# An output projection by seven block products in place of eight, with differences of weight blocks made on GpSimd

## The chip, the cores and the metric

The kernel runs on one core of a Trainium2 chip. The metric is the device time of one execution in microseconds (us); less is better. The engines are named as in the profile: PE (TensorE, matmul; PEld are its weight loads), DVE (VectorE), ACT (ScalarE), POOL (GpSimd), SP (SyncE, which here issues all the DMAs, in program order).

## The reference, cut to what matters

One block of a decoder: x is 1024 tokens by 1024 channels, float32. Two branches, an mLSTM with 4 heads and an S5 state space, are merged by sigmoid gates and go through one output projection, a norm and a residual.

```
xn = rmsnorm(h, norm_pre_g[l])
proj = xn @ w_in[l]
...
y_a = mlstm_branch(...) @ w_a_out[l]
y_b = s5_branch(...) @ w_b_out[l]
g = jax.nn.sigmoid(g_pre.astype(jnp.float32)).astype(h.dtype)
merged = g[..., :D_MODEL] * y_a + g[..., D_MODEL:] * y_b
h = h + rmsnorm(merged @ w_o[l], norm_post_g[l])
```

The last line is what the change touches: merged and w_o are both 1024 by 1024.

## The kernel before, in words

**Products.** All large matmuls are made from float32 values that are split into a high and a low part in a reduced format (fp32r): `dot3` (L181 to L184) issues hi x hi, hi x lo and lo x hi for each 128-deep slice of the contraction. Splitting a value takes a copy on ScalarE (the high part) and a subtraction (the low part). Results gather in PSUM accumulators of 128 by 512: `bank()` hands out 3 of them (tag `pp`), `mbank()` 5 (tag `pm`).

**Weights.** `plan` lists the weight pieces in the order of use. `fetch` loads the next piece into raw tiles (`wr`), `pump` splits one piece into `wh` (ScalarE, L142) and `wl` (L144, on VectorE, or on GpSimd where asked), and `take` hands it over. There are two buffers each of `wr`, `wh` and `wl`.

**Order.** The order of the work is written out by hand. `run` plays one unit: it first issues the DMAs that wait in `pending` (`tick`; `store` puts one there), then the early loads of the next units in `fillers` (as many as `look` says), then the unit's body, and then what an earlier unit put off with `defer`, one unit late. `fill(n)` plays the next n units of `fillers`.

**The S5 output stage** (L780 to L860) has 8 gate units (`glu_unit`, L826: 12 matmuls, tanh on ScalarE, three steps on VectorE) and 16 output units (`yb_unit`, L837: 12 matmuls 128x512 into a `pm` accumulator, then one VectorE step, L844, with a 256 KB tile `aux`, and a store of the product to `gb_d` in DRAM). The tile `aux` is loaded three units ahead (L820) into one of six buffers; it is held until the store of its product has landed.

**The next projection** follows at once: `o_unit` (L895), whose first head makes 264 columns (24 matmuls per unit, `pp` accumulators). ScalarE takes 256 columns (`sow`, L902) and VectorE the other 8 (`gall`, L905), for which it needs two small bias loads (`bif`, L879, L880); these are issued on SyncE behind the last stores of the S5 output stage.

**The merge** (L1410 to L1510) finishes the mLSTM branch's projection and merges: four partial units of 18 matmuls (`ya_unit` with i = 3), sixteen merge units of 6 (`mg_unit`, L1425): one VectorE step on the accumulator (L1432), one that adds the other branch, a copy on ScalarE to `mh`, and one unit late a subtraction on GpSimd to `ml` (L1440). Merge units are named by row block of 128 channels and half of the tokens: (0,1) is block 0, second half.

**The output projection** (`wo_unit`, L1446) takes w_o in four pieces of 256 columns; each piece runs over 8 tiles of 128 tokens, 24 matmuls 128x256 in a unit, 768 in all. The units of the first piece are mixed with the last merge units. Behind each unit ScalarE squares the accumulator (L1460, for the norm), VectorE multiplies by the norm's weight, and in the last piece GpSimd makes the root (L1467, L1468) and VectorE scales and adds the residual (`finish`, L1474, two steps of 128x512), which is stored.

Of the kernel before, what the change touches and what calls it, by code (L numbers as in the profile page):

```python
# [36 lines left out]
def hybrid_block(ctx, tc, x, norm_pre_g, w_in, conv_w, conv_b, w_q, w_k, w_v, b_i, b_f, head_g,  # L37
# [780 lines left out]
    def load_aux(key, src):  # L818
        t = gq.tile([P, 512], F32, tag="aux", bufs=6, name="aux")
        SY.dma_start(t, src)  # L820
# [594 lines left out]
    mh, ml = {}, {}

    def mg_pre(ct, hf):
        rs = slice(ct * P, (ct + 1) * P)
# [4 lines left out]
        maux[ct, hf] = (t1, pr, None)

    def mg_unit(ct, hf):  # L1425
        if "ya3" not in cur:
# [5 lines left out]
        V.scalar_tensor_tensor(t1, t1, 1.0, o, op0=ALU.add, op1=ALU.mult)  # L1432
# [4 lines left out]
        mh[ct, hf] = fp.tile([P, 512], F32R, name=f"mh{ct}{hf}")  # L1437
        ml[ct, hf] = fp.tile([P, 512], F32R, name=f"ml{ct}{hf}")
        A.activation(mh[ct, hf], t1, AF.Copy)  # L1439
        defer(lambda: PL.tensor_tensor(ml[ct, hf], t1, mh[ct, hf].bitcast(F32), op=ALU.subtract))  # L1440

    ob, xres = {}, {}
    sso = fp.tile([P, NCH, 5], F32, name="sso")

    def wo_unit(i, t):
        if t == 0:  # L1446
            cur["wo", i] = take(("wo", i), i > 0)
        if i == 0:
            ob[t] = main.tile([P, D], F32, tag=f"xh{t}", name=f"ob{t}")
            xres[t] = main.tile([P, D], F32, tag=f"xl{t}", name=f"xr{t}")  # L1450
        if i == 1:
            SY.dma_start(xres[t], x[0, t * P:(t + 1) * P, :])
        hf = t // 4
        sl = slice((t % 4) * P, (t % 4 + 1) * P)
        o = bank()
        proj_tm(o[:, :256], lambda k: mh[k, hf][:, sl], lambda k: ml[k, hf][:, sl], cur["wo", i], 0, 256,
                KT)
        cs = slice(256 * i, 256 * (i + 1))
        jk = fp.tile([P, 256], F32, tag="fjk", bufs=1, name="fjk")
        A.activation(jk, o[:, :256], AF.Square, scale=1.0 / 32.0, accum_out=sso[:, t, i:i + 1])  # L1460
        mul(ob[t][:, cs], o[:, :256], gpo[:, cs])
        if i == 2:
            V.tensor_reduce(sso[:, t, 4:5], sso[:, t, 0:3], axis=mybir.AxisListType.X, op=ALU.add)
            V.tensor_scalar(sso[:, t, 4:5], sso[:, t, 4:5], 4.0 * EPS, None, op0=ALU.add)
        if i == 3:
            s = fp.tile([P, 1], F32, tag="fs", bufs=4, name="fs")
            PL.tensor_tensor(s, sso[:, t, 3:4], sso[:, t, 4:5], op=ALU.add)  # L1467
# [75 lines left out]
```

## Time and profile before

| what | us |
|---|---|
| runs | 989.50, 988.57, 987.05 |
| median | 988.57 |
| the profiled execution | 987.63 |
| its span, first to last instruction | 985.9 |

Rows of a timeline give start, duration, engine, line, operation, out<-in with shapes, and in brackets the idle time of the engine just ahead and what ended it. SPq rows are the queue of SyncE: the start is the issue of a DMA, not its landing. Rows of groups give the busy time, the mean of one in ns, and the idle time ahead of them with its releaser.

### The profile page before, as it was taken

The page shows a single profiled execution, that of the slowest core. Times are in us where ns is not written, and L with a number is a line of the kernel's source. Part 1 is how long each engine was busy: PE and PEld are TensorE (multiplying, and loading weights), DVE is VectorE, ACT ScalarE, POOL GpSimd, SP SyncE. Part 2 cuts the span into 40 slices and gives each one's busy share as a digit, 9 for nine tenths or more (in the row PEclk, how much of TensorE's full clock was granted, in tenths as well). Part 3 has the DMA queues.
Part 4 walks back from the last instruction along what each step waited for, and adds up shares of the span by engine and source line. Part 5 has one row for each costly group of instructions (what it writes and reads, how often), then busy time and mean ns, then how long its engine had stood idle before and what let it go on. Part 6 is the DMA issues. An engine that isn't in the chain of part 4 may idle for free.

```text
span 985.9 us, 15233 instructions
## 1 busy us (share of the span) xinstructions
PE 972.8 (99%) x5644; PEld 840.9 (85%) x5644; DVE 621.9 (63%) x1397; ACT 352.9 (36%) x697; POOL 207.1 (21%) x215
## 2 busy tenths in 40 slices
PE   9999999999999999999999999998999999999997
PEld 7888888888887889978998898888988888879997
DVE  5437968879644752444686677747775888664225
ACT  7413132231314421224544445434543452233211
POOL 3013122111112000013111321223222311462002
PEclk9999999999999999999999999999999999999999
DMA  7454323423434566115344254335437895772504
GB/s 257 109 159 150 96 89 99 111 57 110 110 97 166 186 216 229 59 68 148 97 134 152 82 178 124 134 97 177 133 117 226 281 302 191 243 249 90 193 1 172
DMA packets 113722, 145.17 MB, mean 147 GB/s; under 512 B 18888, under 2 KB 71280, under 8 KB 113648
## 3 DMA queue, kind: packets, MB, share of 16 engines
q1 hardware_dynamic: 113648, 144.21, 46.0%
q8 instruction: 44, 0.72, 0.3%
q14 instruction: 30, 0.25, 0.1%
HBM read 98.79 MB, written 45.38 MB: 146 GB/s over the span
## 4 chain that ended last, share of the span: by engine, by line
PE 88%; issue 3%; POOL 3%; DVE 2%; DMA 2%; ACT 1%; SPq 0%; DVEq 0%; POOLq 0%; ACTq 0%
PE pp L182 24%; PE pp L183 23%; PE pp L184 23%; PE pm L184 4%; PE pm L182 4%; PE pm L183 4%; PE pm L1151 1%; POOL wl L144 1%; PE pm L727 1%; PE pm L768 1%; PE pm L767 1%; PE pm L1074 1%; DMA so_d<-sow 1%; POOL ml L1440 1%; POOL t2k L1270 1%
## 5 line engine op out<-in xcount | busy, mean ns | idle before, releaser
L182 PE MATMUL pp<-xh,wh 128*128 128x512 f32 x768 | 306.9, 400 | 0.0
L183 PE MATMUL pp<-xl,wh 128*128 128x512 f32 x768 | 303.8, 396 | 0.0
L184 PE MATMUL pp<-xh,wl 128*128 128x512 f32 x768 | 303.8, 396 | 0.0
L182 PEld LDWEIGHTS pp<-xh,wh 128*128 128x128 f32 x768 | 144.4, 188 | 35.1 <-ACT wt L691 0.8
L184 PEld LDWEIGHTS pp<-xh,wl 128*128 128x128 f32 x768 | 144.4, 188 | 34.6
L183 PEld LDWEIGHTS pp<-xl,wh 128*128 128x128 f32 x768 | 144.5, 188 | 32.4 <-DVE xl L295 0.3
L144 POOL TENSOR_TENSOR wl<-wr,wh 128x1024 fp32r<-128x1024 f32 (+1 forms) x25 | 61.6, 2482 | 229.1 <-ACT wh L142 229.1
L142 ACT ACTIVATE wh<-wr 128x1024 fp32r<-128x1024 f32 (+2 forms) x74 | 71.0, 1006 | 46.5 <-PE pm L183 30.6
L184 PE MATMUL pp<-wh,ml 128*128 128x256 f32 x256 | 72.6, 284 | 1.3 <-POOL ml L1440 1.3
L144 DVE TENSOR_TENSOR wl<-wr,wh 128x1024 fp32r<-128x1024 f32 (+2 forms) x49 | 55.9, 1172 | 27.7 <-ACT wh L142 23.2
L182 PE MATMUL pp<-wh,xh 128*128 128x256 f32 (+1 forms) x256 | 72.3, 282 | 0.6 <-ACT sow L902 0.6
L183 PE MATMUL pp<-wl,mh 128*128 128x256 f32 x256 | 72.5, 283 | 0.0
L182 PE MATMUL pp<-wh,mh 128*128 128x256 f32 x256 | 71.9, 281 | 0.0
L184 PE MATMUL pp<-wh,xl 128*128 128x256 f32 (+1 forms) x256 | 71.8, 281 | 0.0
L183 PE MATMUL pp<-wl,xh 128*128 128x256 f32 (+1 forms) x256 | 71.8, 280 | 0.0
L308 ACT ACTIVATE tg<-pp 128x512 f32<-128x512 f32 x32 | 19.2, 598 | 127.4 <-PE pp L184 89.4
L1048 POOL TENSOR_TENSOR hll<-t2k,hlh 128x512 fp32r<-128x512 f32 x16 | 21.1, 1319 | 182.7 <-ACT hlh L1047 106.0
L184 PEld LDWEIGHTS pp<-wh,ml 128*128 128x128 f32 x256 | 48.1, 188 | 1.7 <-POOL ml L1440 1.7
L182 PEld LDWEIGHTS pp<-wh,mh 128*128 128x128 f32 x256 | 48.7, 190 | 0.5 <-ACT mh L1439 0.4
L182 PEld LDWEIGHTS pp<-wh,xh 128*128 128x128 f32 x256 | 48.1, 188 | 1.2 <-ACT sow L902 1.0
L183 PEld LDWEIGHTS pp<-wl,xh 128*128 128x128 f32 x256 | 48.2, 188 | 0.2
L184 PEld LDWEIGHTS pp<-wh,xl 128*128 128x128 f32 x256 | 48.1, 188 | 0.0
(412 smaller groups left out, 1810.0 us busy)
## 6 DMA issues: line engine op xcount, KB each, us to landing
wr<-in_w_in_dram SPq DMA_DIRECT2D x48, 512.0 KB
t_d<-tg SPq DMA_DIRECT2D x32, 256.0 KB
xt<-in_x_dram SPq DMA_DIRECT2D x8, 512.0 KB
aux<-t_d SPq DMA_DIRECT2D x16, 256.0 KB
gb_d<-aux SPq DMA_DIRECT2D x16, 256.0 KB
so_d<-sow SPq DMA_DIRECT2D x32, 128.0 KB
sz_d<-t2k SPq DMA_DIRECT2D x16, 256.0 KB
cs_d<-t2k SPq DMA_DIRECT2D x16, 256.0 KB
```

Of the source, the lines that this page charges most:

```text
L142: A.activation(hi, raw, AF.Copy)
L144: eng.tensor_tensor(wl[:, k0:k0 + n, c0:c0 + w], raw, hi.bitcast(F32), op=ALU.subtract)
L182: PE.matmul(o, lh, rh, start=first, stop=False)
L183: PE.matmul(o, lh, rl, start=False, stop=False)
L184: PE.matmul(o, ll, rh, start=False, stop=last)
L308: A.activation(t, o, AF.Tanh, scale=0.5)
L727: PE.matmul(o[NS * b2:NS * (b2 + 1), g * P:(g + 1) * P], q["wt"][:, ri, g, NS * b2:NS * (b2 + 1)], ut[b][:, 2 * g + b2, :], start=True, st ...
L767: PE.matmul(o, m0[:, 2 * g + b2, :], ut[b][:, 2 * g + b2, :], start=True, stop=False)
L768: PE.matmul(o, vs[:, b2, g].rearrange("p t n -> p (t n)"), ss_[:, b2, g, :], start=False, stop=True)
L1048: PL.tensor_tensor(lo, acc, hi.bitcast(F32), op=ALU.subtract)
L1074: PE.matmul(pm[:, 256 * k:256 * k + 256], wt[:, e, 256 + P * k:256 + P * k + P], wt[:, e, 0:256], start=e == 0, stop=e == 1)
L1151: PE.matmul(sc[:, :P], k_[:, m, sl], q_[:, m, sl], start=m == 0, stop=m == 1)
```

## The change

w_o and the merged rows are cut in 2 by 2 blocks of 512, and the output is made from seven products of blocks (p1 to p7, Strassen's scheme in Winograd's form), each of 512 tokens by 512 channels by 512: 4 units of 12 matmuls 128x512, 336 in all, the last unit in two halves of 256 columns. It needs four combinations of weight blocks and four of blocks of merged rows.

The weight combinations are made in the S5 output stage in 16 steps (`wo_load`, `wo_comb`), each a quarter by a quarter of the four blocks: two loads of `wc` (512-byte rows), four subtractions 128x128 on GpSimd, two stores to `wt_d`; `wc` has two buffers, and `aux` goes from six to five. A step is put into each of the last four gate units and each of the output units as long as there are any. The pieces are later loaded as weights.

The combinations of merged rows are made on VectorE in `s_pair`, as soon as both units of a pair are there; the low parts of merged rows go from GpSimd to VectorE. The outputs are assembled from the products by VectorE additions; the squares read these sums from SBUF; `finish` is put off by one unit, other than for the last one.

```diff
-    for i in range(4):
-        plan(("wo", i), [w_o[0][:, 256 * i:256 * i + 256]], KT, 256)
+    wo11, wo12 = w_o[0][0:512, 0:512], w_o[0][0:512, 512:1024]
+    wo21, wo22 = w_o[0][512:1024, 0:512], w_o[0][512:1024, 512:1024]
+    for n, src in (("p1", wo11), ("p2", wo21), ("p6", wt_d[1, 1]), ("p7", wt_d[0, 1]), ("p4", wt_d[1, 0]),
+                   ("p5", wt_d[0, 0]), ("p3", wo22)):
+        plan(n, [src], 4, 512)
...
-        t = gq.tile([P, 512], F32, tag="aux", bufs=6, name="aux")
+        t = gq.tile([P, 512], F32, tag="aux", bufs=5, name="aux")
...
+    def wo_load():
+        if wsteps:
+            j, q = wsteps.popleft()
+            t = gq.tile([P, 2, 2, P], F32, tag="wc", bufs=2, name="wc")
+            for a in range(2):
+                r = 512 * a + P * j
+                SY.dma_start(t[:, a], w_o[0][r:r + P, :].rearrange("p (b c) -> p b c", b=2)[:, :, P * q:P * q + P])
+            wcomb.append((j, q, t))
+
+    def wo_comb():
+        if wcomb:
+            j, q, t = wcomb.popleft()
+            sub_ = lambda o, a, b: PL.tensor_tensor(o, a, b, op=ALU.subtract)
+            b11, b12, b21, b22 = t[:, 0, 0], t[:, 0, 1], t[:, 1, 0], t[:, 1, 1]
+            sub_(b11, b12, b11)
+            sub_(b12, b22, b12)
+            sub_(b22, b22, b11)
+            sub_(b21, b21, b22)
+            for a in range(2):
+                store(wt_d[a][:, P * j:P * j + P, P * q:P * q + P].rearrange("b p c -> p b c"), t[:, a])
...
     def yb_unit(i, m, hf):
...
+        wo_comb()
+        wo_load()
         o = mbank()
...
-        defer(lambda: PL.tensor_tensor(ml[ct, hf], t1, mh[ct, hf].bitcast(F32), op=ALU.subtract))
+        if b != 2:
+            A.activation(ah[b][:, j], t1, AF.Copy)
+            defer(lambda: tt(al[b][:, j], t1, ah[b][:, j].bitcast(F32), ALU.subtract))
+        if hf:
+            pair.setdefault(j, []).append(ct)
+            if len(pair[j]) == 2:
+                defer(lambda: s_pair(j))
...
+    def s_pair(j):
+
+        a11, a12, a21, a22 = mrow(j, 0), mrow(4 + j, 0), mrow(j, 1), mrow(4 + j, 1)
+        tt(a22, a21, a22, ALU.add)
+        tt(a21, a11, a21, ALU.subtract)
+        tt(a11, a22, a11, ALU.subtract)
+        tt(a12, a12, a11, ALU.subtract)
+        defer(split_1(2, j, a11, V))
...
+    def tail_col(b, q, stash, o):
+        c = cb_[b][q]
+        t = 4 * (b // 2) + q
+        g_ = cb_["g"][:, 512 * (b % 2):512 * (b % 2) + 512]
+        tt(c, stash[:, q], o, ALU.add)
+        square(c, t, b % 2)
+        mul(c, c, g_)
...
+    def p5(q):
...
+        mul_unit(5, sv[1], o, q)
+        tail_col(3, q, cb_["u3"], o)
+        tt(cb_["u2"][:, q], cb_["u2"][:, q], o, ALU.add)
+        s = rms(4 + q, 1)
+        defer(lambda: finish(4 + q, s))
...
+    fill(2)
+    pump()
+    fill(2)
...
+    go(p1, 0)
+    fill(2)
+    go(p1, 1)
+    fill(2)
+    fill(2)
+    go(p1, 2)
+    pump()
+    for f, q in [(p1, 3)] + [(f, q) for f in (p2, p6, p7, p4, p5, p3) for q in range(4)]:
+        go(f, q)
+    flush2()
```

Three places in the order of the instructions. The first is SyncE's queue in the S5 output stage: `gb_d<-aux` stores a product, `aux<-t_d` loads the tile for a unit four further on. Before:

```order
L82 DMA gb_d<-aux 128x512
L820 DMA aux<-t_d 128x512
L82 DMA gb_d<-aux 128x512
L820 DMA aux<-t_d 128x512
L82 DMA gb_d<-aux 128x512
```

And now:

```order
L83 DMA wt_d<-wc 128x2x128 x2
L83 DMA gb_d<-aux 128x512
L824 DMA aux<-t_d 128x512
L838 DMA wc<-in_w_o_dram 128x2x128 x2
L83 DMA wt_d<-wc 128x2x128 x2
L83 DMA gb_d<-aux 128x512
L824 DMA aux<-t_d 128x512
L838 DMA wc<-in_w_o_dram 128x2x128 x2
```

Between one aux load and the next stand two loads of `wc`, two stores of `wt_d` and the store of a product, where only that store stood.

The second is VectorE's queue in the last part of the merge. Before, the end of the merge units around the first units of the projection (`ft` are merged rows, `fpa` the other branch):

```order
L1432 SCALAR_TENSOR_TENSOR ft<-ft,pp 128x512
L505 TENSOR_TENSOR ft<-ft,fpa 128x512
L1432 SCALAR_TENSOR_TENSOR ft<-ft,pp 128x512
L505 TENSOR_TENSOR ft<-ft,fpa 128x512
L505 TENSOR_TENSOR ob_8928<-pp,gpo 128x256
L1432 SCALAR_TENSOR_TENSOR ft<-ft,pp 128x512
```

And now, up to the split of p2's weights and the first sum of p2 (`r_8765`, `r_8766`, `r_8773` and `r_8774` hold the four blocks of merged rows, `s2l` the low part of a combination, `a22l` that of a block, `c_9181` an output block, `m` p1's product):

```order
L1515 TENSOR_TENSOR s2l_8952<-r_8765,s2h_8950 128x512
L509 TENSOR_TENSOR a22l<-r_8774,a22h 128x512
L509 TENSOR_TENSOR r_8774<-r_8773,r_8774 128x512
L509 TENSOR_TENSOR r_8773<-r_8765,r_8773 128x512
L509 TENSOR_TENSOR r_8765<-r_8774,r_8765 128x512
L509 TENSOR_TENSOR r_8766<-r_8766,r_8765 128x512
L145 TENSOR_TENSOR wl<-wr,wh 128x1024 x2
L1515 TENSOR_TENSOR s2l_8952<-r_8765,s2h_8950 128x512
L509 TENSOR_TENSOR c_9181<-m_9025,pm 128x512
```

The split of p2's weights stands behind the last set of four combinations and the low parts ahead of it.

The third is the end of VectorE's queue. Before, the last two token tiles (`ob` is the output, `fs` the root, `xr` the residual):

```order
L505 TENSOR_TENSOR ob_9171<-pp,gpo 128x256
L1474 SCALAR_TENSOR_TENSOR ob_9171<-ob_9171,fs,xr_9172 128x512 x2
L505 TENSOR_TENSOR ob_9201<-pp,gpo 128x256
L1474 SCALAR_TENSOR_TENSOR ob_9201<-ob_9201,fs,xr_9202 128x512 x2
L1539 UNCONDITIONAL_BRANCH
```

And now, p3's last unit in two halves and what follows (`c_9182` and `c_9629` are the two column halves of the output):

```order
L509 TENSOR_TENSOR c_9629<-u_9269,pm 128x256
L509 TENSOR_TENSOR c_9629<-c_9629,gpo 128x256
L509 TENSOR_TENSOR sso<-sso 128x1
L509 TENSOR_TENSOR c_9629<-u_9269,pm 128x256
L509 TENSOR_TENSOR c_9629<-c_9629,gpo 128x256
L1563 SCALAR_TENSOR_TENSOR c_9182<-c_9182,fs,xr_9451 128x512
L1563 SCALAR_TENSOR_TENSOR c_9629<-c_9629,fs,xr_9451 128x512
L1563 SCALAR_TENSOR_TENSOR c_9182<-c_9182,fs,xr_9450 128x512
L1563 SCALAR_TENSOR_TENSOR c_9629<-c_9629,fs,xr_9450 128x512
```

Two scalings stood last and now four do: those of token tile 3 (`xr_9451`), then those of tile 2, which was put off.

More of the change, by code (lines that the diff above doesn't have):

```diff
@@ L72, in hybrid_block @@
     nm_d = dscr.tile([32, P], F32, name="nm_d")
+    wt_d = dscr.tile([2, 2, 512, 512], F32, name="wt_d")
     ident = main.tile([P, P], F32, name="ident")
@@ L1436, in mg_unit @@
             V.scalar_tensor_tensor(t1, pr, 0.25, t1, op0=ALU.mult, op1=ALU.add)
[L1437 to L1467, printed above, removed]
-            PL.tensor_tensor(s, s, halfm[:, 0:1], op=ALU.pow)
-            finish(t, s)
@@ new lines, in hybrid_block, with mul_unit, junk, square @@
+    sso = fp.tile([P, NCH, 4], F32, name="sso")
+    cb_ = {}
+    wcur = {}
+    xres = {}
+    def mul_unit(w, lhs, o, tq, cs=slice(0, 512)):
+        hi, lo = lhs
+        wh, wl = wcur[w]
+        sl = slice(tq * P, (tq + 1) * P)
+        for k in range(4):
+            dot3(o, hi[k][:, sl], lo[k][:, sl], wh[:, k, cs], wl[:, k, cs], k, k == 0, k == 3)
+    def junk():
+        return fp.tile([P, 512], F32, tag="fpa", bufs=6, name="junk")
+    def square(src, t, i):
+        n = src.shape[1]
+        A.activation(junk()[:, :n], src, AF.Square, scale=1.0 / 32.0, accum_out=sso[:, t, i:i + 1])
@@ L1493, in hybrid_block, with load_res, p1 @@
-    n_hf = len(fillers) - n_ya
-    for ct in range(2, 6):
-        mgf(ct, 1)
+            V.scalar_tensor_tensor(c, c, s, xres[t][:, qs_], op0=ALU.mult, op1=ALU.add)
+            store(out[0, t * P:(t + 1) * P, qs_], c)
+    def load_res(t, tag):
+        xres[t] = main.tile([P, D], F32, tag=tag, name=f"xr{t}")
+        store(xres[t], x[0, t * P:(t + 1) * P, :])
+    rows4 = lambda a: [a[:, k] for k in range(4)]
+    def p1(q):
+        if q == 0:
+            wcur[1] = take("p1", False)
+            cb_["m1"] = block("a9", "m1")
+        o = mbank()
+        mul_unit(1, (rows4(ah[0]), rows4(al[0])), o, q)
+        A.copy(cb_["m1"][:, q], o)
@@ new lines, in p2 @@
+    def p2(q):
+        if q == 0:
+            wcur[2] = take("p2", False)
+            c11 = [main.tile([P, 2, 512], F32, tag=f"xh{6 + i}", name=f"c11{i}") for i in range(2)]
+            cb_[0] = [c11[i // 2][:, i % 2] for i in range(4)]
+        o = mbank()
+        mul_unit(2, (rows4(ah[1]), rows4(al[1])), o, q)
+        tt(cb_[0][q], cb_["m1"][:, q], o, ALU.add)
+        square(cb_[0][q], q, 0)
+        if q == 0:
+            pump()
+            cb_["g"] = main.tile([P, D], F32, tag="xl6", name="gpo")
+            store(cb_["g"], norm_post_g[0].partition_broadcast(P))
+        if q >= 2:
+            split_s(3, V)
@@ new lines, in p5 @@
+    def p5(q):
+        if q == 0:
+            wcur[5] = take("p5", False)
+            cb_[3] = rows4(block("a10", "c22"))
+            for t in range(4):
+                V.tensor_scalar(sso[:, t, 3:4], sso[:, t, 0:1], 4.0 * EPS, None, op0=ALU.add)
+        o = mbank()
+        mul_unit(5, sv[1], o, q)
[3 more added lines that the diff above has]
+        defer(lambda: finish(4 + q, s))
+        if q == 0:
+            pump()
```

169 lines of the change are left out of this document (129 added, 40 removed).

## The prediction

> **What bounds the kernel now.** I read the page first: busy shares, then the chain that ended last.
>
> ```profile
> span 985.9 us, 15233 instructions
> PE 972.8 (99%) x5644; PEld 840.9 (85%) x5644; DVE 621.9 (63%) x1397; ACT 352.9 (36%) x697; POOL 207.1 (21%) x215
> PE 88%; issue 3%; POOL 3%; DVE 2%; DMA 2%; ACT 1%; SPq 0%; DVEq 0%; POOLq 0%; ACTq 0%
> L1048 POOL TENSOR_TENSOR hll<-t2k,hlh 128x512 fp32r<-128x512 f32 x16 | 21.1, 1319 | 182.7 <-ACT hlh L1047 106.0
> L184 PE MATMUL pp<-wh,ml 128*128 128x256 f32 x256 | 72.6, 284 | 1.3 <-POOL ml L1440 1.3
> ```
>
> TensorE has work all the time and carries 88% of the chain, so a matmul taken away is worth its pitch, and any wait that reaches TensorE is worth its full length. The output projection itself waits only 1.3 us. The profiled execution took 987.63 us, 1.73 more than its span; the median of the runs, 988.57, lies 0.94 above it. All walks below are in the time of the span.
>
> Next I read the timelines of the stages that the change touches: the output projection, the merge ahead of it, and the S5 output stage.
>
> **The projection's matmuls.** First ScalarE's squares, one per unit of the projection before, then VectorE's products of two neighbouring S5 output units, whose 12 matmuls have the shape of the new ones.
>
> ```profile
> 971.33 0.38 ACT L1460 ACTIVATE fjk<-pp 128x256 f32<-128x256 f32 x1 [2.40 <-PE pp L184]
> 974.21 0.38 ACT L1460 ACTIVATE fjk<-pp 128x256 f32<-128x256 f32 x1 [2.41 <-PE pp L184]
> ...
> 380.65 0.69 DVE L844 SCALAR_TENSOR_TENSOR aux<-aux,pm 128x512 f32<-128x512 f32 x1 [2.03 <-DMA gb_d<-aux]
> 383.37 0.69 DVE L844 SCALAR_TENSOR_TENSOR aux<-aux,pm 128x512 f32<-128x512 f32 x1 [2.03 <-PE pm L184]
> ```
>
> A unit of 24 matmuls 128x256 takes 2.88 us; there are 32, so 92.2. A unit of 12 matmuls 128x512 takes 2.72; 27 of these and one unit in two halves (2.88) make 76.3. TensorE's gain is **15.8 us**, if nothing waits.
>
> **The merge.** The lo parts go from GpSimd to VectorE, and four combinations of row blocks come on top.
>
> ```profile
> 846.23 0.48 PE L182 MATMUL pp<-xh,wh 128*128 128x512 f32 x1
> ...
> 885.34 0.39 PE L184 MATMUL pp<-xh,wl 128*128 128x512 f32 x1
> ...
> 887.44 0.40 PE L184 MATMUL pp<-xh,wl 128*128 128x512 f32 x1
> 872.62 2.36 DVE L144 TENSOR_TENSOR wl<-wr,wh 128x1024 fp32r<-128x1024 f32 x2 [5.81 <-ACT wh L142]
> ...
> 886.53 0.69 DVE L1432 SCALAR_TENSOR_TENSOR ft<-ft,pp 128x512 f32<-128x512 f32 x1 [0.53 <-PE pp L184]
> 887.25 0.69 DVE L505 TENSOR_TENSOR ft<-ft,fpa 128x512 f32<-128x512 f32 x1
> 887.93 0.69 DVE L1432 SCALAR_TENSOR_TENSOR ft<-ft,pp 128x512 f32<-128x512 f32 x1
> 888.65 0.69 DVE L505 TENSOR_TENSOR ft<-ft,fpa 128x512 f32<-128x512 f32 x1
> ```
>
> The first row is the merge's first matmul. The next two stand nine matmuls apart: 0.233 each, so a partial unit (18) takes 4.2 and a merge unit (6) 1.4. A dependent 128x512 step costs VectorE 0.72 from start to start, a merge unit 1.4, a lo part about 0.65, a weight split 2.36 (the row with the 5.81 us idle ahead of it: that idle is what the lo parts may eat unseen).
>
> TensorE alone would start p1 at 846.2 + 4 x 4.2 + 10 x 1.4 = 877.0. The split of p1 is asked for behind one more merge pair, seven lo parts (4.6) stand ahead, and I put its end at 878.2: 1.2 lost. From there VectorE is never idle. Up to the first step of the merge unit (0,1) it has four merge units (5.6), three lo parts, two sets of four combinations (2.9 each) and an s2 lo part with its copy on ScalarE: 15, so 893.1 to 893.8. That step frees one of three accumulators, and the unit (5,1) needs it; TensorE arrives at 890.6. Another 3.2 lost. TensorE then reaches p2 at 900.7. VectorE has the rest of (0,1), three merge units, four lo parts and two sets ahead of p2's split, and the first half of that split: 14.7, so p2 starts at about **908.5**, 7.8 lost. Together 12; p2's first unit ends at 910.8. Both bounds: nothing lost at p2 if VectorE's steps overlap as the 0.61 between some of its starts suggests and the split slips ahead (gain of 7.8), and 3 more if each of the four s2 copies adds its 0.7.
>
> **The projection's end.** From p2 on VectorE has less than 2.72 us per unit until p5. p5's first unit ends on TensorE 16 units later, 910.8 + 43.5 = 954.3. In p5 each unit gives VectorE three steps of 0.7 and, one unit late, two scalings; in p3 two steps and two scalings.
>
> ```profile
> 979.97 0.38 ACT L1460 ACTIVATE fjk<-pp 128x256 f32<-128x256 f32 x1 [2.40 <-PE pp L184]
> ...
> 980.80 0.54 POOL L1468 TENSOR_TENSOR fs<-fs,halfm 128x1 f32<-128x1 f32 x1
> ...
> 981.37 1.42 DVE L1474 SCALAR_TENSOR_TENSOR ob<-ob,fs,xr 128x512 f32<-128x512 f32 x2 [0.47 <-POOL fs L1468]
> ```
>
> Before, the last accumulator was ready at 979.9, two scalings (1.42) followed square and root, and the span ended 3.1 us behind them. After: p5 is 4 x 2.1 + 3 x 1.42 + 2.36 (p3's split) = 15.0 and p3's first three units 3 x 2.83 = 8.5; so VectorE is through these at 977.8, while TensorE has been done with everything since 973.4. The last unit adds 1.9 for two halves, about 0.8 for square and root, and four scalings (2.8), since unit 3 is scaled ahead of the deferred unit 2: 983.4. With the 3.1 the span would end at 986.5, against 985.9. The projection's 15.8 is used up: **+0.6 us**, with -7 and +3 as ends.
>
> **The S5 output stage.** Here the change adds 16 steps: 2 loads, 4 subtractions on GpSimd, 2 stores. All issue on SyncE's queue, in one order with the gate loads (`aux<-t_d`) and the gated stores (`gb_d<-aux`). Rows of SyncE's timeline in time order, then one of VectorE's and two of ScalarE's; two early SyncE rows; two rows of the list of DMA issues; and the row of a 25 us window (the last three columns are clock, DMA share, GB/s).
>
> ```profile
> 350.85 2.06 SPq L124 DMA_DIRECT2D wr<-in_w_in_dram  x4
> 353.00 0.55 SPq L82 DMA_DIRECT2D gb_d<-aux  x1
> ...
> 354.61 0.59 SPq L820 DMA_DIRECT2D aux<-t_d  x1
> ...
> 359.90 0.47 SPq L82 DMA_DIRECT2D gb_d<-aux  x1
> ...
> 364.21 0.32 SPq L820 DMA_DIRECT2D aux<-t_d  x1
> ...
> 376.68 0.32 SPq L820 DMA_DIRECT2D aux<-t_d  x1
> 377.05 7.35 SPq L82 DMA_DIRECT2D gb_d<-aux  x4
> 384.44 0.43 SPq L879 DMA_DIRECT2D bif<-in_b_i_dram  x1
> 387.74 0.18 DVE L505 TENSOR_TENSOR gall<-pp,bif 128x8 f32<-128x8 f32 x1 [1.14 <-DMA bif<-in_b_f_dram]
> 386.26 0.38 ACT L902 ACTIVATE sow<-pp 128x256 f32<-128x256 f32 x1 [1.11 <-PE pp L184]
> 389.16 0.38 ACT L902 ACTIVATE sow<-pp 128x256 f32<-128x256 f32 x1 [2.52 <-PE pp L184]
> 75.42 0.34 SPq L82 DMA_DIRECT2D u_d<-uc  x1
> 78.09 0.36 SPq L82 DMA_DIRECT2D ut<-u_d  x1
> u_d<-uc SPq DMA_DIRECT2D x4, 512.0 KB
> gb_d<-aux SPq DMA_DIRECT2D x16, 256.0 KB
> 355.00:380.00 25.00, 25.00 (x112) 20.69 (x112) 9.03 (x12) 2.06 (x2) 0.00 (x0) 1.00 0.94 311
> ```
>
> Count the aux loads from 0: no. 13 is issued at 354.61, the last (no. 23) at 376.68, 2.2 us apart each. The chain behind no. 23 leads to TensorE: it lands, the last product is made, its store goes out, then the two bias loads, then the first `gall`, which frees one of three accumulators of the next projection. Before, `gall` comes 3.3 behind the issue of the bias loads and the fourth unit of that projection starts at 391.9 (its units end just ahead of ScalarE's copies, 2.9 us apart, the second at 389.16), so nothing waits.
>
> After, a step on SyncE is: two wt stores, a gated store, an aux load, two wc loads. There are two wc tiles, so the loads wait until the stores just ahead have landed, and the stores wait for loads of a step earlier and four subtractions on the same tile. A 512 KB store took at most 2.7 us from issue to landing where nothing else moved (75.42 to 78.09). In this stage a 256 KB store took 4.3 (359.90 to 364.21, where the load reuses its buffer). A 128x128 subtraction is an estimate from the 128x512 row (1319 ns): a quarter to a half, four together about 2.0. The ring of two steps is store landing + load landing + subtractions: (2.7 + 2.7 + 2.0)/2 = 3.7 us per step with the first price, (4.3 + 4.3 + 2.0)/2 = 5.3 with the second; store landing and two issues alone give 3.5. A step moves 1.05 MB, 3.4 us at the 311 GB/s of the window. I take **4.1**, nearer to the unloaded row, since the queue now empties itself at each wait.
>
> No. 13 comes at about 359.5: ahead of it the fourth tile's wt stores queue behind four weight loads (1.06 MB, started by 351.6), land at about 357.2, and two wc loads, two wt stores and a gated store follow. No. 23 then is issued at 359.5 + 10 x 4.1 = 400.5. Landing 2.5, product and store 1.1, biases to `gall` 3.3: 407.4 against 391.9, a stall of **15.5 us** on TensorE; 9.5 at 3.5 per step, 27.5 at 5.3, none at 2.5 or less.
>
> ```profile
> 847.75 2.68 DVE L505 TENSOR_TENSOR t2k<-t2k,cz 128x512 f32<-128x512 f32 x1
> 851.13 0.69 DVE L505 TENSOR_TENSOR t2k<-t2k,cz 128x512 f32<-128x512 f32 x1
> 847.49 2.40 POOL L144 TENSOR_TENSOR wl<-wr,wh 128x1024 fp32r<-128x1024 f32 x1 [6.71 <-ACT wh L142]
> 286.00:288.00 2.00, 2.00 (x10) 1.63 (x9) 0.00 (x0) 0.00 (x0) 0.00 (x0) 1.00 0.75 136
> ```
>
> The same VectorE step takes 2.68 beside a GpSimd subtraction and 0.69 without one, so the subtractions slow the four gate units of the S5 stage, whose chain (3.1 us per unit on VectorE) hides most of it. I cost it at nothing, and at 2 us where the first gated store comes late. The Trainium skill says in "SBUF — State Buffer", section "SBUF: two separate sides", that VectorE with two SBUF inputs and GpSimd hold the port pair in turn, the other fully blocked; the trace agrees (2.68 beside 0.69), and by the rule taken strictly the 2 us would be owed.
>
> The last row is a stretch of 512-byte-row stores: 136 GB/s at a share of 0.75, so 181 at full share (from 16 partitions, which makes it a far row). At that rate a step's stores land 1.3 us later and a step costs about 4.7, which is inside the two ends. The Trainium skill's "DMA: Bandwidth & Descriptors", section "Specifications", puts line rate at 512 bytes and above; by that the 1.3 falls away and 4.1 stays.
>
> **Sum.** 987.63 + 15.5 + 0.6 = 1003.7 in the profiled execution's own time; 0.94 up to the median's level gives 1004.7, rounded to **1005**.
>
> **The rivals.**
> First, the slow end: landings as in the loaded row, 5.3 per step, stall 27.5, and 2 more in the merge. For it speaks that the added transfers themselves load the window that already had a share of 0.94. 987.6 + 27.5 + 2.6 + 0.9 = about **1018**.
> Second, the detour is hidden: SyncE goes on at 2.5 per step or faster. For it: landings in quiet stretches are short and gate loads run three units ahead. Against it: three landings and a subtraction in series. Then only +0.6 is left: **989**.
> Third, faster: the detour is hidden as before, and p2's split gets through by 900.7, before TensorE arrives. The point that decides is whether VectorE's queue of 14.7 us in front of that split shrinks by 7.8; for it, before's VectorE has starts 0.61 apart; against it, the combinations depend on one another, at 0.72. 987.6 + 0.6 - 7.8 + 0.9 = **981**.
>
> **Chances and range.** Forecast 0.58 (995 to 1012: steps of 3.5 to 4.7, the merge's ends); slow end 0.13; hidden 0.15; faster 0.14. A difference within 0.3% (3 us) is about what a measurement of this kernel cannot tell from no change. So faster 0.14, same 0.14 (most of the second rival), slower 0.72. The range leaves out the third rival and the far half of the first: 986 to 1016.
>
> **What the changed profile would show.** Right: SyncE's wc loads stand 3.5 to 4.7 us apart between 360 and 400 and wait on `wt_d<-wc`; the fourth 128x264 projection unit waits on `gall` and bias loads until about 407; p2's first matmul waits on VectorE's split by 5 us or more; VectorE ends some 10 us behind TensorE. Wrong: steps of 2.5 us or an idle TensorE under 3 us near 390 take the stall away; a p2 that starts within 2 us of p1's end, or TensorE ending later than 980 less the stall's shift, refutes the merge walk. Matmul units of 2.8 us or more instead of 2.72 would cost 2 us over 27.

## The result, and the profile after

The changed kernel takes 1031.44 us (median of 4 runs, 1029.73 to 1032.41) against 987.95 for the kernel before in the same comparison: a ratio of 1.0437, 95% interval 1.0416 to 1.0458. It is 43.5 us slower; the forecast was 16 or so, and its range ended at 1016.

The page of the changed kernel: span, busy shares, and the chain by engine.

```profile
span 1029.1 us, 14603 instructions
PE 966.5 (94%) x5224; PEld 816.8 (79%) x5224; DVE 667.3 (65%) x1442; ACT 363.7 (35%) x689; POOL 242.9 (24%) x275
PE 75%; DMA 7%; DVE 6%; issue 4%; POOL 3%; ACT 2%; SPq 2%; DVEq 0%; POOLq 0%; ACTq 0%
```

TensorE's share of the chain fell from 88% to 75%; transfers and VectorE took its place. The waits of TensorE in the changed kernel, each with its total, how often, and the longest:

```profile
PE pp L183 <- DVE gall L509: 19.1, 1, 19.1
PE pm L183 <- DVE c L509: 12.3, 1, 12.3
PE pm L183 <- ACT wh L143: 7.2, 2, 6.9
PE pm L183 <- DVE aux L879: 6.4, 5, 2.7
PE pp L183 <- DVE r L1495: 2.7, 1, 2.7
```

The fourth lies in the S5 output stage and the first at its end, where the next projection starts; the others lie in the merge and the output projection. How much each side costs is read from where two marks of the program come. The first mark is ScalarE's fourth copy in the next projection: it starts at 395.01 before. The second is the end of the span. ScalarE's timeline after, and VectorE's at the same place:

```profile
425.59 0.39 ACT L937 ACTIVATE sow<-pp 128x256 f32<-128x256 f32 x1 [0.87 <-PE pp L185]
420.28 0.25 DVE L509 TENSOR_TENSOR gall<-pp,bif 128x8 f32<-128x8 f32 x2 [2.00 <-DMA bif<-in_b_f_dram]
```

So the program was 30.6 us late there (425.59 against 395.01), and 43.2 at its end (1029.1 against 985.9): **30.5 us belong to the S5 output stage and 12.7 to merge, projection and end.** The forecast had 15.5 and 0.6.

SyncE's queue in the S5 output stage, from aux load no. 13 (363.19) over one step, then the place at which two weight loads stand between, and the last aux load (no. 23):

```profile
363.19 0.45 SPq L824 DMA_DIRECT2D aux<-t_d  x1
364.73 1.20 SPq L838 DMA_DIRECT2D wc<-in_w_o_dram  x2
366.02 1.06 SPq L83 DMA_DIRECT2D wt_d<-wc  x2
367.13 0.50 SPq L83 DMA_DIRECT2D gb_d<-aux  x1
367.67 0.47 SPq L824 DMA_DIRECT2D aux<-t_d  x1
...
390.00 0.45 SPq L824 DMA_DIRECT2D aux<-t_d  x1
391.46 1.20 SPq L838 DMA_DIRECT2D wc<-in_w_o_dram  x2
392.76 1.10 SPq L125 DMA_DIRECT2D wr<-in_w_in_dram  x2
...
400.06 1.20 SPq L838 DMA_DIRECT2D wc<-in_w_o_dram  x2
...
403.02 0.45 SPq L824 DMA_DIRECT2D aux<-t_d  x1
...
411.64 0.43 SPq L824 DMA_DIRECT2D aux<-t_d  x1
```

The ten steps from no. 13 to no. 23 took 48.4 us. Eight of them took 3.9 to 5.1, 4.43 on average, of which 3.2 are issuing (1.20 + 1.06 + 0.50 + 0.45); the rest is mostly the wait of the `wc` loads for the two stores ahead of them to land. With the weight loads between, the two steps from 390.00 to 403.02 took 13.0.

The end of the program: VectorE in one unit of p5, from one first sum to the next; then the last unit, with TensorE's start of its second half and VectorE's last scalings.

```profile
999.19 0.68 DVE L509 TENSOR_TENSOR c<-u,pm 128x512 f32<-128x512 f32 x1
1000.73 0.69 DVE L509 TENSOR_TENSOR c<-c,gpo 128x512 f32<-128x512 f32 x1 [0.85 <-ACT junk L1551]
1001.33 0.68 DVE L509 TENSOR_TENSOR u<-u,pm 128x512 f32<-128x512 f32 x1
1001.93 1.41 DVE L1563 SCALAR_TENSOR_TENSOR c<-c,fs,xr 128x512 f32<-128x512 f32 x2
1003.26 0.68 DVE L509 TENSOR_TENSOR c<-u,pm 128x512 f32<-128x512 f32 x1
...
1017.71 0.42 DVE L509 TENSOR_TENSOR c<-u,pm 128x256 f32<-128x256 f32 x1
1018.18 0.58 PE L183 MATMUL pm<-wh,s4h 128*128 128x256 f32 x1 [12.33 <-DVE c L509]
1023.33 2.74 DVE L1563 SCALAR_TENSOR_TENSOR c<-c,fs,xr 128x512 f32<-128x512 f32 x4 [0.71 <-POOL fs L1556]
```

The product with the norm's weight works in place on `c`, which ScalarE is squaring (`junk`); VectorE stands idle for 0.85 until that read is done, and a unit takes 4.07 instead of the 3.5 that I had summed. The second half of the last unit starts only when VectorE has read the first half; both lie in one accumulator tile.

### The profile page after: what moved, and what is told of

It reads as the page before. It is cut to its first block, busy times and chain, and to the rows that moved or that the text cites. A ratio compares the mean times of both kernels' runs of the same rounds, so it can differ in the third digit from the quotient of the medians.

```text
span 1029.1 us, 14603 instructions
## 1 busy us (share of the span) xinstructions
PE 966.5 (94%) x5224; PEld 816.8 (79%) x5224; DVE 667.3 (65%) x1442; ACT 363.7 (35%) x689; POOL 242.9 (24%) x275
## 4 chain that ended last, share of the span: by engine, by line
PE 75%; DMA 7%; DVE 6%; issue 4%; POOL 3%; ACT 2%; SPq 2%; DVEq 0%; POOLq 0%; ACTq 0%
PE pp L183 19%; PE pp L184 18%; PE pp L185 18%; PE pm L184 4%; PE pm L185 4%; PE pm L183 4%; DMA wt_d<-wc 3%; DMA wc<-in_w_o_dram 2%; POOL wc L844 1%; DVE r L509 1%; DVE c L509 1%; PE pm L1186 1%; POOL wl L145 1%; DVE c L1563 1%; SPq L838 1%
## 5 line engine op out<-in xcount | busy, mean ns | idle before, releaser
L183 PE MATMUL pp<-xh,wh 128*128 128x512 f32 x736 | 294.1, 400 | 2.7 <-DVE r L1495 2.7
L184 PE MATMUL pp<-xl,wh 128*128 128x512 f32 x736 | 291.0, 395 | 0.0
L185 PE MATMUL pp<-xh,wl 128*128 128x512 f32 x736 | 290.9, 395 | 0.0
L143 ACT ACTIVATE wh<-wr 128x1024 fp32r<-128x1024 f32 (+2 forms) x80 | 77.3, 1009 | 64.2 <-DMA wr<-in_w_in_dram 38.8
L183 PE MATMUL pp<-wh,xh 128*128 128x256 f32 (+1 forms) x256 | 73.2, 286 | 19.8 <-DVE gall L509 19.1
L145 DVE TENSOR_TENSOR wl<-wr,wh 128x1024 fp32r<-128x1024 f32 (+2 forms) x55 | 65.0, 1215 | 24.3 <-ACT wh L143 19.8
L312 ACT ACTIVATE tg<-pp 128x512 f32<-128x512 f32 x32 | 19.1, 598 | 127.4 <-PE pp L185 84.4
L844 POOL TENSOR_TENSOR wc<-wc 128x128 f32<-128x128 f32 x64 | 37.7, 590 | 61.3 <-DMA wc<-in_w_o_dram 56.6
L879 DVE SCALAR_TENSOR_TENSOR aux<-aux,pm 128x512 f32<-128x512 f32 x16 | 10.7, 685 | 48.9 <-DMA aux<-t_d 41.0
L1063 DVE SCALAR_TENSOR_TENSOR t2k<-pp,par,t2k 128x511 f32<-128x511 f32 (+2 forms) x48 | 35.7, 744 | 5.1 <-ACT t2k L1056 4.6
L1239 ACT ACTIVATE cth<-ct 128x516 fp32r<-128x516 f32 x28 | 17.8, 637 | 53.2 <-DVE ct L1229 49.1
L1159 POOL TENSOR_TENSOR q<-hlh,hll 128x512 f32<-128x512 f32 x16 | 21.9, 1389 | 49.5 <-DVE q L509 39.5
```

Of the source, the lines that this page charges most:

```text
L143: A.activation(hi, raw, AF.Copy)
L145: eng.tensor_tensor(wl[:, k0:k0 + n, c0:c0 + w], raw, hi.bitcast(F32), op=ALU.subtract)
L183: PE.matmul(o, lh, rh, start=first, stop=False)
L184: PE.matmul(o, lh, rl, start=False, stop=False)
L185: PE.matmul(o, ll, rh, start=False, stop=last)
L312: A.activation(t, o, AF.Tanh, scale=0.5)
```

## The experiments

The theory after the result: the detour is dear only because of its place in SyncE's order, and the later part is dear because of the order in VectorE's queue, not of its matmuls. Rivals: the subtractions on GpSimd, plain bandwidth, five aux buffers in place of six, and that the two parts of the change slow each other. Times are medians. "Before" is the kernel before as it ran in the same comparison. Two edited kernels from different comparisons are set against each other by their distances from it.

**The detour alone.** The kernel before with `wo_load` and `wo_comb` in its S5 output stage, as in the change:

```diff
         t2 = aux.pop((1, ct, hf))
+        wo_comb()
+        wo_load()
```

> The kernel before with nothing but the weight detour put into its S5 output stage (16 steps of 2 loads, 4 subtractions, 2 stores, and five aux buffers in place of six); the differences that it stores are used by nobody. Between the kernel before and the changed kernel the fourth copy of the next projection's first head came 30.6 us later (395.01 to 425.59), so if the two parts of the change do not depend on each other, this kernel takes 988 + 30.5 = 1018.5 us (theory A: everything lost up to there is the detour's). Rival: half or more of it belongs to something else of the change, then below 1005.

1018.68 us, 30.3 more than before (ratio 1.0303, 1.0273 to 1.0333). This is the 30.5 that the marks gave to the S5 output stage, so that side is the detour's, its five aux buffers included.

**Without subtractions.**

```diff
-            sub_(b11, b12, b11)
-            sub_(b12, b22, b12)
-            sub_(b22, b22, b11)
-            sub_(b21, b21, b22)
```

> The same, with the GpSimd subtractions left out (loads and stores stay, the stored blocks are plain copies). Theory A: SyncE's own work sets the pace, some 3.3 us of issuing per step and about 1.1 us of waiting for a store to land, and a store that waits for GpSimd is rare: 1015 to 1019 us. Rival B: the ring store, load, subtraction sets it, then each pair of steps is 2.1 us shorter, a step 3.4 us, and 10 us come off: about 1008 us or less.

1017.35, 1.3 less than with them; the 95% intervals of the two (1.0260 to 1.0320, and 1.0273 to 1.0333) overlap. GpSimd's work is not the cost, neither in the ring nor by holding VectorE up; the slower VectorE steps beside it are hidden.

**The transfers on other queues.**

```diff
-                SY.dma_start(t[:, a], w_o[0][r:r + P, :]...)
+                PL.dma_start(t[:, a], w_o[0][r:r + P, :]...)
...
-                store(wt_d[a][:, ...]..., t[:, a])
+                PL.dma_start(wt_d[a][:, ...]..., t[:, a])
```

> The detour with all its loads and stores issued on GpSimd's queue instead of SyncE's, stores right behind the subtractions. Theory A (the place in SyncE's order is the cost, by issuing and by waiting): the gate loads come as before and TensorE doesn't wait, 988 to 992 us. Rival C (the 1.05 MB per step against some 310 GB/s, 3.4 us): gate loads are late all the same, 997 us or more.

1024.13, slower than on SyncE, and 32 us over the end of what theory A expected. The wait at `gall` did shrink, and another wait took its place. TensorE's waits in this kernel:

```profile
PE pm L963 <- POOL tri L913: 23.6, 1, 23.6
PE pp L183 <- DVE gall L506: 5.9, 1, 5.9
```

The end of the detour in GpSimd's timeline:

```profile
449.57 1.46 POOL L846 DMA_DIRECT2D wt_d<-wc  x2
451.02 0.22 POOL L912 MEMSET tri<- 128x128 f32 x1
```

The wait for `gall` fell to 5.9 (it was 19.9 in the detour alone), for the aux loads came every 2.8 us (no. 13 at 361.42, no. 23 at 389.29; 2.2 before). But a pair of transfers takes GpSimd 1.45 us to issue, its steps went on until 451, and a constant that the next stage needs (`tri`) was queued behind them: 23.6 us of waiting. With five aux buffers and no detour (below) this wait is 0.3, so some 5.6 of the 5.9 are left to what the detour adds besides its place on SyncE: its traffic, or its steps on GpSimd. Which of them is not shown.

> The detour with its loads and stores issued on ScalarE's queue. Theory A: the gate loads on SyncE come as before; ScalarE now waits for GpSimd and for landings, at some 4 us per step, and the copies that free the accumulators of the gate units and of the next projection stand behind these: between 990 and 1008 us, with TensorE's waits named by ScalarE. Rival C (bandwidth): gate loads late, VectorE waiting for aux loads by 3 us and more each, as in the changed kernel.

1042.35, far over the 1008 that I had allowed. ScalarE's queue at the end of this stretch (ACTq rows are issues on it):

```profile
400.30 1.21 ACTq L833 DMA_DIRECT2D wc<-in_w_o_dram  x2
407.06 2.06 ACT L143 ACTIVATE wh<-wr 128x1056 fp32r<-128x1056 f32 x2 [46.28 <-DMA wt_d<-wc]
```

The 46.3 us are not one wait: issuing does not count as busy, and in this time ScalarE went through the `wc` loads of eight steps (360.44 to 405.51), 5.2 to 7.8 us from one to the next instead of the 4 that I had allowed. The split of the next weights stood behind all of them, and TensorE waited up to 24.1 us at one place. Of bandwidth the run tells nothing.

**Transfers on SyncE that need not wait for each other** (no subtractions, stores from a tile `wz` that is filled once, loads into one that nobody reads):

```diff
-                store(wt_d[a]..., t[:, a])
+                store(wt_d[a]..., wz[:, a])
```

> The kernel before with the detour's transfers on SyncE in the same order and number, but free of each other: the stores read one tile that is filled once, the loads go into another that nobody reads, and there are no subtractions. What is left of a step is SyncE's issuing (1.20 + 1.06 + 0.50 + 0.45 = 3.2 us in the changed kernel's rows) and the transfers. If the ring store, landing, load was what made a step 4.4 us (my prediction's mechanism), a step now takes 3.2 to 3.4 us and 10 to 12 us come off the 1018.7 of the detour: 1005 to 1009. Rival: bandwidth sets the step, and the time stays above 1014.

1009.37, 9.3 less than the detour: just above the end of what I expected. SyncE's queue over its shortest step:

```profile
375.88 0.40 SPq L821 DMA_DIRECT2D aux<-t_d  x1
376.38 1.20 SPq L835 DMA_DIRECT2D wc<-in_w_o_dram  x2
377.62 1.11 SPq L83 DMA_DIRECT2D wt_d<-wz  x2
378.83 0.45 SPq L83 DMA_DIRECT2D gb_d<-aux  x1
379.38 0.39 SPq L821 DMA_DIRECT2D aux<-t_d  x1
```

This step takes 3.5 us, and 3.2 of them are issuing. The average from no. 13 (359.07) to no. 23 (401.62) is 4.3, against 4.8 in the detour alone. So the ring that I had made the mechanism carries a third of the cost; two thirds (21 us over before) stay with no ring at all, the five aux buffers among them. Within these, issuing is seen in the rows; how much more the traffic adds (the DMA share was 0.95 from 380 to 400) was not separated.

**Five aux buffers.**

```diff
-        t = gq.tile([P, 512], F32, tag="aux", bufs=6, name="aux")
+        t = gq.tile([P, 512], F32, tag="aux", bufs=5, name="aux")
```

> The kernel before with five aux buffers in place of six and nothing else. The prediction gave this part no cost. In o1, which has no detour but kept five buffers, TensorE waited 2.1 us for the first head's small columns. Theory: 990 to 991.5 us, so some 3 us of the 30 belong to the buffers; rival: the same as before, and o1's wait came from elsewhere.

991.22, 2.9 more (ratio 1.0027, 1.0017 to 1.0037). Not free, as I had taken it. In its trace load no. 13 is issued at 359.67 and no. 23 at 384.47 (354.61 and 376.68 before): with no detour at all, the chain behind no. 23 starts 7.8 us later, and more than half of that is still hidden.

**Seven products without the detour.**

```diff
-    for n, src in (("p1", wo11), ("p2", wo21), ("p6", wt_d[1, 1]), ("p7", wt_d[0, 1]), ("p4", wt_d[1, 0]),
-                   ("p5", wt_d[0, 0]), ("p3", wo22)):
+    for n, src in (("p1", wo11), ("p2", wo21), ("p6", wo12), ("p7", wo21), ("p4", wo22),
+                   ("p5", wo11), ("p3", wo22)):
```

> The changed kernel without the detour: the four difference pieces are replaced by plain blocks of w_o, so its output is not the block's. From the changed kernel's trace 12.7 us of its 43.2 belong to merge, projection and end. Theory A (the two parts add): 988 + 12.7 = 1000.7 us, 998 to 1003. Rival (the later part was slowed by the detour, by the clock or by late weights): 990 to 996.

1003.35, 15.1 more than before (ratio 1.0166, 1.0140 to 1.0192). Less the 2.9 for the five buffers that it keeps, 12.2 are left for the output side, against 12.7 read from the two traces. The parts add: 30.3 and 15.1, with the buffers counted once, make 42.5, against 43.5 for the whole change.

**The product put off by one unit:**

```diff
-        mul(c, c, g_)
+        defer(lambda: mul(c, c, g_))
```

> o1 with one edit: the product with the norm's weight, in place on the tile that ScalarE squares, is put off by one unit, so VectorE no longer stands idle for that read (0.79 to 0.85 us in each of 11 units of p4, p5 and p3). If VectorE's queue sets the end, as I hold, 8 to 9 us come off but no more than up to where TensorE leads again: 992 to 994 us against o1's 1000.7. Rival: the end is set by TensorE and the last unit, nothing comes off.

996.13, 7.2 less than o1, a little under the 8 to 9 expected. VectorE's timeline, one unit of p5:

```profile
965.14 0.68 DVE L508 TENSOR_TENSOR c<-u,pm 128x512 f32<-128x512 f32 x1
965.73 0.68 DVE L508 TENSOR_TENSOR u<-u,pm 128x512 f32<-128x512 f32 x1
966.33 0.69 DVE L508 TENSOR_TENSOR c<-c,gpo 128x512 f32<-128x512 f32 x1
966.93 1.41 DVE L1533 SCALAR_TENSOR_TENSOR c<-c,fs,xr 128x512 f32<-128x512 f32 x2
968.26 0.68 DVE L508 TENSOR_TENSOR c<-u,pm 128x512 f32<-128x512 f32 x1
```

The same five steps, 3.12 us instead of 4.07, with no idle time between.

**An accumulator for each half of the last unit.**

```diff
+            if i:
+                o = mbank()
             mul_unit(3, sv[4], o[:, cs], q, cs)
```

> o1 with one edit: the second half of p3's last unit gets an accumulator of its own. In the changed kernel its first matmul stood 12.3 us behind VectorE's read of the first half. Theory: the halves waited because they shared one tile; then 2.5 to 3.5 us come off at the end (997 to 998 against 1000.7), as the second half's product is ready when VectorE gets there. Rival: the wait costs nothing, since VectorE is late anyway: 0.

1001.69, 1.7 less than o1, and that is not clear of the scatter (ratios to before 1.0127 to 1.0158, and 1.0140 to 1.0192 for o1). The 12.3 us of waiting are gone from the trace and little or nothing comes off: VectorE is late anyway, as the rival said.

**The split of p2's weights ahead of p1's third unit.**

```diff
-    go(p1, 2)
-    pump()
+    pump()
+    go(p1, 2)
```

> o1 with one edit: the split of p2's weights is asked for ahead of p1's third unit, in front of the last set of combinations. Theory: TensorE's wait for p2's weights (6.9 us on ScalarE's copy in the changed kernel) goes, and some 2 of half clock behind it; but if VectorE's queue sets the end of the program, the 4 to 8 us at p2 come back only in part: 993 to 1000 us. Rival: p2's start counts in full, 992 to 993.

998.00, 5.4 less than o1; the wait for p2's weights is 2.0 instead of 6.8. The time lies where the theory had it, and not at the rival's 992 to 993.

**The three together, and more.** o5 also empties the list of put-off steps between the two halves, and o6 gives half of four splits to GpSimd:

```diff
             if i == 0:
                 tt(sso[:, q, 3:4], sso[:, q, 3:4], sso[:, q, 1:2], ALU.add)
+                flush2()
...
-            pump()
+            pump(pl=True)
```

> o1 (seven products without the detour, plain blocks in place of differences) with the three edits together: products with the norm's weight put off, own accumulator for the last half, p2's split asked for earlier; and the put-off scaling of the unit before is done between the two halves of the last unit. Alone the three took 7.2, 1.7 and 5.3 us off o1's 1003.35, the fourth should take the last two scalings (1.4) and a product (0.7) out of the end. If they add: 1003.4 - 14.2 - 2 = 987 us, a tie with the kernel before. Rival: VectorE's queue in front of p5 is the common bound and p2's 5.3 are no longer felt or felt double: 990 to 993, or 984.

990.94 (ratio to before 1.0032, 1.0019 to 1.0045), 12.0 less than o1. The single gains add to 14.3; with the fourth edit 16 were expected. So they overlap in part; that this is because VectorE's queue stands behind each of them fits the traces but was not tested by itself.

> o5 with half of each weight split for p7, p4, p5 and p3 moved from VectorE to GpSimd (1.2 us less on VectorE for each, 2.5 more on GpSimd). Theory (VectorE's queue sets the end from p4 on): 2 to 3 us come off against o5. Rival: the two engines hold each other up on SBUF, 0 or slower.

992.61, no gain on o5 (its ratio to before is 1.0030 to 1.0060, which overlaps o5's): the rival. Its trace shows why. While GpSimd worked, four of VectorE's products `c<-c,gpo` took 2.29, 1.13, 1.13 and 2.89 us where the undisturbed ones took 0.68; these 4.7 us more use up the four halves of splits, some 1.1 us each, that VectorE was spared.

**The detour moved to the stage of the S5 scan**, a step every two units:

```diff
+        for f in beat:
+            f()
         new = len(stage2)
         body()
...
+        if n >= 0 and n % 2 == 0:
+            wo_load()
+        if n >= 0 and n % 2 == 1:
+            wo_comb()
```

> The changed kernel whole, its output the block's again, with the 16 steps of the detour moved out of the S5 output stage: one step every two units of the gate projections that run beside the S5 scan (the stage where the DMA share of before was 0.2 to 0.4), store one unit behind the subtractions, load two units behind the store; aux back to six buffers. Theory (the detour cost 28 to 30 us only because of its place on SyncE ahead of the gate loads): as fast as o1, 1003 us (1001 to 1006). Rival: the detour has a price of its own wherever it stands (DMA, or GpSimd against VectorE): 1008 or more.

1002.15, 29.1 less than the changed kernel, with the same loads, subtractions and stores; some 2.9 of these are the sixth aux buffer, which c1 has again. The fourth copy of the next projection comes at 396.79, so up to there the detour costs 1.8 us in its new place (30.6 in the old one). This shows that the place is the cost; how the cost in the old place divides into issuing and traffic stays open. One wait of 1.6 us is left ahead of the gate units (TensorE at 313.27, for a step of VectorE); in the stretch where the detour stood, TensorE is busy throughout (350 to 380; columns: TensorE, its weight loads, VectorE, ScalarE, GpSimd, clock, DMA share, GB/s):

```profile
350.00:380.00 30.00, 30.00 (x134) 24.82 (x134) 14.16 (x19) 4.36 (x5) 0.00 (x0) 1.00 0.82 266
```

> c1 with o5's edits, its output the block's: if c1 equals o1, this equals o5, 985 to 990 us, at best a tie with the kernel before (988.2); by the rival of c1 5 us more.

989.25 (ratio 1.0016, 1.0007 to 1.0026): 42 us under the changed kernel and a little above the one before.

**The merge's waits.** c3 puts the sets of combinations off by one more unit, c4 also asks for p2's split inside the last merge unit.

```diff
-                defer(lambda: s_pair(j))
+                defer(lambda: s_pair(j), 2)
```

> c2 (detour moved, p2's split earlier, products put off, own accumulator) with the sets of four combinations put off by one more unit, so that merge unit (0,1) gets its VectorE step ahead of the second set. TensorE's wait for that accumulator (2.7 us) should go without another in its place: 985.5 to 987.5 us, 1 to 2.5 less than c2's 989.25 and a little under the kernel before. Rival: the sets now stand in front of p2 or p6 and the wait comes back there: 989 or more.

988.48 (ratio 1.0005, 0.9996 to 1.0014). The wait for the accumulator is gone and one for p2's weights has come in its place; TensorE's waits from the merge on:

```profile
PE pm L183 <- ACT wh L143: 5.7, 2, 5.4
```

And c4:

```diff
+        if hf and ct == 5:
+            pump()
         if hf:
             pair.setdefault(j, []).append(ct)
...
-    pump()
     go(p1, 2)
```

> c3 with p2's split asked for inside the last merge unit, ahead of the third set of combinations and its copy on ScalarE. In c3 the wait that left the accumulator came back as 5.4 us in front of p2's weights, whose copy stood on ScalarE behind that of a combination. Theory: this order leaves neither wait, and 4 to 6 us come off c3's 988.5: 982.5 to 985, under the kernel before by 0.3 to 0.6%. Rival: VectorE's queue from p5 on, about as long as TensorE's, sets the end alone: 986.5 or more.

987.96 (ratio 0.9999, 0.9990 to 1.0007). Its waits of TensorE in the same part:

```profile
PE pm L183 <- ACT wh L143: 3.6, 2, 3.3
PE pm L184 <- DVE wl L145: 2.9, 4, 0.8
```

The forecast gain did not come; the time is where the rival put it. The traces of c2, c3 and c4 show two parts. Up to p5 TensorE still leads, and its waits in merge and projection change place without getting less: 5.1, 7.0 and 6.5 us in all. p5's first sum comes at 955.4, 954.2 and 955.0. From there on VectorE works almost without a gap, TensorE is done 10 us ahead of VectorE's last step, and the end comes 32.3 to 32.4 us behind p5's first sum in each of the three. So VectorE sets the length of the last part; an earlier p5 would still count, and no order tried gave one. The fastest version found is a tie with the kernel before; none beats it.

## Why the prediction was wrong, point by point

**Direction and place: right. Size: wrong, by 26 us.** The chain from the last aux load through the biases to `gall` and a full set of accumulators is the one that the trace shows, and it is the longest wait.

**The S5 output stage, 15.5 forecast, 30.5 measured.** The step that failed is "No. 23 then is issued at 359.5 + 10 x 4.1 = 400.5": it was issued at 411.6. Term by term:

- No. 13 was issued at 363.2 instead of 359.5 (3.7 more). The `wt` stores behind the four weight loads had landed only by 360.2, when the next `wc` loads went out, not at 357.2.
- The ten steps took 48.4 instead of 41 (7.4 more). Two of them, with two weight loads between, took 13.0 instead of 8.2, and the `wc` loads behind them waited until 400.06; this is 4.8 of the 7.4. I had seen such loads ahead of no. 13 and not the later ones. The other eight took 4.43 instead of 4.1.
- From no. 23 to `gall` it was 8.6 instead of 6.9 (1.7 more).

These make 28.3 of stall. The rest is the clock, which was no term of the sum (below).

"I take 4.1, nearer to the unloaded row, since the queue now empties itself at each wait" came near the 4.43, but for the wrong reason, and so by luck. The ring of two landings and the subtractions did not set the step: in the rows the `wt` stores go out right behind the `wc` loads (366.02 behind 364.73 + 1.20), and without subtractions, in s2, only 1.3 us came off. What a step holds is 3.2 us of issuing and 1.2 more, mostly a wait for the stores. I had counted two issues at most and left the rest of SyncE's own time as hidden in the landings. A short-row load takes 0.60 us to issue, about the longest of the plain transfers in the rows of before (0.32 to 0.59), and four such transfers come on top in each step. The stall passed the slow end (27.5) without its steps of 5.3: the average of the ten was 4.8.

**Terms at nothing.** "I cost it at nothing, and at 2 us where the first gated store comes late" held: without the subtractions 1.3 us come off, not clear of the scatter. Four subtractions took 2.4 us (590 ns each) where 2.0 were estimated. On the Trainium skill's "SBUF — State Buffer", section "SBUF: two separate sides": VectorE's steps beside the subtractions did stretch (the split 2.36 to 2.62 us in the S5 stage), far from the 2.68 for 0.69 of the rows in the prediction, and little of it reached the kernel's time. The five aux buffers were not costed at all and are 2.9 us by themselves. By the Trainium skill's "DMA: Bandwidth & Descriptors", section "Specifications", short rows of 512 bytes go at line rate; no run here separates rate from issuing, and it is the issuing that is seen in the rows. The 1.3 us by which stores at the lower rate would land later do not come out of the prediction's own numbers: the 0.26 MB of a step's stores take 1.4 us at 181 GB/s and 0.8 at 311. They were no term of the sum.

**The merge, right in place and size.** Forecast waits 1.2, 3.2 and 7.8; measured 1.1 (0.3 and 0.8 for the two parts of the split), 2.7, and 7.4 (6.9 and 0.5). The 6.9 end on ScalarE's copy of p2's weights and not on VectorE's split: the copy stands behind that of a combination, which waits for VectorE. The 0.5 are the second part, and there the split ends it.

```profile
936.94 0.63 ACT L1514 ACTIVATE s2h<-r 128x512 fp32r<-128x512 f32 x1 [2.47 <-DVE r L509]
937.48 1.99 ACT L143 ACTIVATE wh<-wr 128x1024 fp32r<-128x1024 f32 x2
938.57 0.80 PE L183 MATMUL pm<-wh,a12h 128*128 128x512 f32 x1 [6.86 <-ACT wh L143]
```

Then the clock: most of p2's first unit ran at half of it, and the unit ended at 944.2, 2.9 us later than forecast (910.8 + 30.5). The 910.8 itself is a slip of 0.4: 908.5 + 2.72 is 911.2.

**The end, 9 us short.** From the end of p2's first unit to the end of the span the prediction has 75.7 us; it took 84.9. The steps that failed are "From p2 on VectorE has less than 2.72 us per unit until p5" and "In p5 each unit gives VectorE three steps of 0.7 and, one unit late, two scalings". Both count VectorE's work and not its wait for ScalarE's read of the tile it works in place on: 0.79 to 0.85 in each of 11 units of p4, p5 and p3; o2 gives 7.2 back. In p4 two products took 1.53 as well, beside GpSimd:

```profile
983.94 5.54 POOL L1515 TENSOR_TENSOR s4l<-r,s4h 128x512 fp32r<-128x512 f32 x4 [9.82 <-ACT s4h L1514]
987.04 0.67 DVE L509 TENSOR_TENSOR c<-u,pm 128x512 f32<-128x512 f32 x1
988.50 1.53 DVE L509 TENSOR_TENSOR c<-c,gpo 128x512 f32<-128x512 f32 x1 [0.79 <-ACT junk L1551]
```

So p5's first sum came 2.5 us late, p5 took 2.1 more than forecast, p3's first three units 1.9 more, and the last unit with its scalings 2.8 more (8.4 instead of 5.6), with the second half behind VectorE's read of the first. With p2's split earlier and the in-place wait, the shared accumulator and the late scaling gone, in c2 to c4, p5's first sum stands at 954.2 to 955.4 and the end 32.3 behind it, where the prediction had 954.3 and 32.2. So its length for the last part fits a kernel that doesn't wait there. That the start agrees as well is partly chance: the waits ahead of it (5.1 to 7.0) are shorter than the 12 forecast, while the moved detour and the clock took time that the sum did not have.

**The rivals.** Hidden and faster both needed steps of 2.5 us or less and fell with that. Slow named the right stage, and its time, 1018, was still 13 us short.

## What to carry to other kernels

Price transfers that are added to a queue issued in order by three numbers: the issuing time of each, the landing that the next one waits for, and every other transfer that comes between; then ask who waits for what stands behind, and look for a stage where nobody does. There the same work cost 26 to 29 us less. A product less on TensorE is worth its pitch only if the engine that assembles the result has room: 15.8 us of matmuls were saved, and in the best order found TensorE ended less than 6 us earlier than before (974.2 against 979.9), because of its waits, the clock behind them and the detour; and VectorE, with its additions and scalings, needed 10 us more behind it (3 before).

When a step works in place on a tile that another engine is reading, put another step between (7.2 us here). Halves of a unit with accumulators of their own took away a wait of 12.3 us, but hardly any time while another engine was later still.

## What the runs showed of the hardware

After long waits TensorE started again at half clock. In the changed kernel it stood still from 931.7 to 938.6, and the granted clock fell between 936 and 938, and rose again at 943 to 944, some 5 us after work had come back (columns: TensorE, its weight loads, VectorE, ScalarE, GpSimd, clock, DMA share, GB/s):

```profile
934.00:936.00 2.00, 0.00 (x0) 0.00 (x0) 1.90 (x3) 0.48 (x2) 0.00 (x0) 1.00 0.00 0
936.00:938.00 2.00, 0.00 (x0) 0.00 (x0) 1.57 (x3) 1.06 (x2) 0.00 (x0) 0.64 0.00 0
942.00:943.00 1.00, 1.00 (x3) 0.76 (x3) 0.00 (x0) 0.00 (x0) 0.00 (x0) 0.50 1.02 395
944.00:946.00 2.00, 2.00 (x11) 1.65 (x10) 0.69 (x1) 0.86 (x3) 0.00 (x0) 1.00 0.21 79
```

Matmuls of 0.23 pitch went at 0.43 meanwhile, which added some 2 us to this wait; the 19.1 us wait in the S5 output stage cost the same 2 on top (30.6 of delay against 28.6 until TensorE's restart at 420.5). The 2.7 us of waiting at the merge, ended at 924.6, left the clock at 1.00 in the stretches of 2 us around it. In c4 a wait of 3.3 us that ended at 903.3, with one of 0.8 a matmul later, was followed by a clock of 0.50 from 906 to 908.

Beside GpSimd's subtractions in p4 (1.3 us and more each), VectorE's products of two SBUF tiles took 1.53 us instead of 0.69, and its sums with an accumulator as one input stayed at 0.67 (the rows above).
